# A second buffer for the first-key one-hots, paid for with the tiles of transposed expert numbers

## Chip, core and metric

The kernel runs on one core of one Trainium2 chip. The metric is the device time of one execution in microseconds. The engines are named as in the profile: PE (matrix products), DVE (the vector engine), ACT (activations), POOL (a general engine, which here also issues the gathers), SP (which issues most of the plain loads and stores).

## What is computed

One transformer block for 1024 tokens of width 1024 (and 16 meta tokens): a convolution branch and a latent attention branch, then a channel mixer that picks experts by product keys, then a final norm. Nearly all that matters here is the mixer:

```
s = jnp.einsum('chpd,hpnd->chpn', q, keys)        # two lists of 128 scores per head
sv, si = lax.top_k(s, K)                          # K = 16, 8 heads
...
eidx = jnp.take_along_axis(cidx.reshape(C, PEER_HEADS, K * K), sel, axis=-1)
g = jax.nn.softmax(top_s, axis=-1)
u = u_tab[eidx]                                   # 16384 experts of 1024 numbers
act = jax.nn.gelu(jnp.einsum('chkd,cd->chk', u, xb))
w = g * act
return jnp.einsum('chk,chkd->cd', w, v_tab[eidx])
```

So each token picks 8 x 16 = 128 of the 16384 experts. An expert's number is 128 times its first key plus its second key.

## The kernel before

The 1024 tokens are eight chunks of 128. The mixer is computed in two ways side by side.

**Gather path, chunks 0 to 3.** For each of the 128 picks of a token POOL gathers a row of `u_tab` per token (tile `ug`, 512 KB, line 696), and DVE takes its dot product with the token (`ujunk`, L699). Then rows of `v_tab` are gathered (tile `vg`): for chunks 0 to 2 token by token, summed by PE (`gv`, L736 and L740), for chunk 3 pick by pick, summed by DVE (`ht`, L711 and L713). There are 512 gathers of `u` and 512 of `v`. They are steps of one stream that runs beside the rest of the program.

**Dense path, chunks 4 to 7.** PE computes all 16384 experts for these 512 tokens: `pa` (L180, from `u_t`) and `pv` (L180, into `acc` by DVE at L857). This is the dense part, the second half of the execution. It needs the weights of all experts for each token, most of them zero, and those are made by the **expansion** before it.

**The expansion** (function `expand`, run once per dense chunk, E0 to E3) goes through a chunk in 4 quarters of 32 tokens, and a quarter in 4 pieces of 8 (`r0` = 0, 8, 16, 24), 64 pieces in all. A piece makes four tiles of 128 x 1024 half-precision numbers: `two` (one-hots of the second key), `one` (one-hots of the first key), `ah` = `one` times the high part of the weight, `al` = `one` times the low part. DVE makes them, except that `al` of the pieces with `r0` 8 and 24 is made by POOL. PE multiplies `ah` and `al` with `two` into `pg`, ACT copies that out (`st`), and SP stores it (`g_d`), where the dense part reads it (`gt`). `two`, `ah` and `al` have two buffers each; `one` has one. So the next piece's `one` waits until `ah` and `al` of this piece have been made, on POOL where POOL makes `al`.

**What sets the order.** The program is written as a list of steps (`ORDER`: B attention, C output mix and key scores, S and T the choice of experts, E expansion, G and U gathers and first dense work, D dense part). A scheduler places every instruction by a simulated time when the kernel is built, and so fixes each engine's order; on the chip each engine works through its own list strictly in order and waits by semaphores. What stands between two instructions in a list therefore depends on what the scheduler thought would be ready. POOL's gathers stand in the same list as its `al`, and DVE's dot products in the same list as `two`, `one`, `ah` and the additions into `acc`.

In names such as `one4_1_24` and `vg3_108` the first number is the chunk; then come quarter and `r0`, or the number of the gather.

The function `turn` makes `eT`, a chunk's expert numbers with tokens along the free axis (512 bytes per partition). Chunks 0 to 2 keep it, since their gathers of `v` read it; for chunks 4 to 7 only the two instructions behind it read it. Chunk 3 has none.

Of the kernel before, what the change touches and what calls it, by code (L numbers as in the profile page):

```python
# [17 lines left out]
I32 = mybir.dt.int32  # L18
# [7 lines left out]
P = 128  # L26
# [36 lines left out]
GATHER = [0, 1, 2, 3]  # L63
# [21 lines left out]
def trunk_kernel(ctx, tc, x, meta, g_mix, w_ab, w_lat, g_q, w_uq, g_kv, w_ukv, conv_w, conv_b,  # L85
# [5 lines left out]
    const = ctx.enter_context(tc.tile_pool(name="const", bufs=1))  # L91
# [3 lines left out]
    def bank(name, shape=(P, 512), tag="c"):  # L95
        pool, n, t = banks[tag]
        return pool.tile(list(shape), F32, name=name, tag=t, bufs=n)
# [59 lines left out]
    def transpose_to(dst, src, m):  # L157
        PE.transpose(dst, src, ident[:m, :m])
# [504 lines left out]
    def turn(c):  # L663

        if c in VROWS:
            return
        ef, g = picks[c]
        tp = bank(f"et{c}", (P, 4, P), "s" if c in DENSE else "c")
        transpose_to(tp[:, 0], ef, P)
        eT = const.tile([P, P], I32, name=f"eT{c}", tag="eT", bufs=5)  # L670
        V.tensor_copy(eT, tp[:, 0])
        if c in GATHER:
            chunks[c] += (eT,)
        else:
            transpose_to(tp[:, 1], g.rearrange("p h k -> p (h k)"), P)
            t = sel.tile([P, 4, P], F16, name=f"gd{c}", tag="gd", bufs=len(DENSE))
            A.activation(t[:, 0], tp[:, 1], AF.Copy, scale=GSCALE)
            V.scalar_tensor_tensor(t[:, 1], tp[:, 1], GSCALE, t[:, 0], op0=OP.mult, op1=OP.subtract)
            ii = sel.tile([P, 2, P], I32, name=f"ii{c}", tag="ii", bufs=1)
            V.tensor_scalar(ii[:, 0], eT, 7, None, op0=OP.logical_shift_right)  # L680
            V.tensor_scalar(ii[:, 1], eT, NK - 1, None, op0=OP.bitwise_and)
            V.tensor_copy(t[:, 2:4], ii)
            chunks[c] = t
# [77 lines left out]
    def expand(ci):  # L761

        c = DENSE[ci]
        t = chunks[c]
        for q in range(P // TG):
            st = [ex.tile([P, NK // 2, TG], F32, name=f"st{c}_{q}_{i}", tag="st", bufs=STB) for i in range(2)]
            for r0 in range(0, TG, TH):
                sh = [P, TH // 2, NK, 2]

                def col(r):  # L770
                    cv = t[:, r, q * TG + r0:q * TG + r0 + TH].rearrange("p (a b) -> p a b", b=2)
                    return cv[:, :, None, :].broadcast_to(sh)
                one, two, ah, al = [ex.tile(sh, F16, name=f"{n}{c}_{q}_{r0}", tag=n, bufs=b)
                                    for n, b in (("one", 1), ("two", 2), ("ah", 2), ("al", 2))]
                V.tensor_tensor(two, io[:, None].broadcast_to(sh), col(3), op=OP.is_equal)  # L775
                V.tensor_tensor(one, io[:, None].broadcast_to(sh), col(2), op=OP.is_equal)  # L776
                V.tensor_tensor(ah, one, col(0), op=OP.mult)  # L777
                (G if r0 // TH in ALP else V).tensor_tensor(al, one, col(1), op=OP.mult)
                for r in range(0, TH, 4):
                    pg = bank(f"pg{c}_{q}_{r0}_{r}", (P, 4, NK), "bs"[r // 4 % 2])  # L780
                    for k in range(4):
                        a, b = divmod(r + k, 2)
                        PE.matmul(pg[:, k], two[:, a, :, b], ah[:, a, :, b], start=True, stop=False)  # L783
                        PE.matmul(pg[:, k], two[:, a, :, b], al[:, a, :, b], start=False, stop=True)  # L784
                    for i in range(2):
                        A.activation(st[i][:, :, r0 + r:r0 + r + 4].rearrange("p a b -> p b a"),  # L786
                                     pg[:, :, i * NK // 2:(i + 1) * NK // 2], AF.Copy, scale=1.0 / GSCALE)
            for i in range(2):
                gs = slice(i * NK // 2 // NG, (i + 1) * NK // 2 // NG)
                nc.sync.dma_start(g_d[gs, :, ci * (P // TG) + q].rearrange("g p r -> p g r"),  # L790
                                  st[i].rearrange("p (g a) t -> p g (a t)", a=NG))
# [103 lines left out]
    for t in tops[0]:  # L895
        select(*t)
        turn(t[0])
# [16 lines left out]
    for step in ORDER.split():  # L914
# [8 lines left out]
        elif step[0] == "T":  # L923
            for t in tops[i]:
                turn(t[0])
        elif step[0] == "X":
            bp_ctx.close()
            ex = ex_ctx.enter_context(tc.tile_pool(name="ex", bufs=1, side="right", **RW))
            io = ex.tile([P, NK, 2], F16, name="io")
            G.iota(io, pattern=[[1, NK], [0, 2]], base=0, channel_multiplier=0, allow_small_or_imprecise_dtypes=True)  # L930
        elif step[0] == "Y":
            cp_ctx.close()
            dx = ctx.enter_context(tc.tile_pool(name="dx", bufs=1, **RW))
            XD = (dx.tile([P, KD, ND], F32R, name="xdh"), dx.tile([P, KD, ND], F32R, name="xdl"))
            du = ctx.enter_context(tc.tile_pool(name="du", bufs=1, **RW))
            ges = []
        elif step[0] == "N":
            dense_x()
        elif step[0] == "U":
            ges += [dense_u(k, lambda n: bank(n)) for k in range(i)]  # L940
        elif step[0] == "E":
            expand(i)
        elif step[0] == "D":
            ex_ctx.close()
            sel_ctx.close()
            ps_ctx.close()
            dense()
        else:
            for _ in range(i):
                next(steps)  # L950
# [54 lines left out]
```

## Time and profile before

| | |
|---|---|
| Median of the runs | 2932.6 us (2932.31 to 2934.2, 3 runs) |
| The profiled execution's own time | 2917.6 us |
| Its span, first to last instruction | 2915.8 us |
| Busy: PE / DVE / POOL / ACT | 2495.5 / 2286.2 / 1637.0 / 992.8 us |
| Expansion, first to last of its tiles on DVE | 934.5 to about 1366 us |
| Dense part, first `pv` to last | 1401 to about 2886 us |

All stretches below are microseconds from the start of that span. The span is 1.8 us shorter than the execution's own time, and that is 15 us shorter than the median of the runs; a change is worked out against the profiled execution and then carried to the median. In a row of a timeline the first two numbers are start and duration, and the brackets at the end give the time that the engine sat idle before it and what released it. In a row of waits the numbers are total us, times, and longest.

### The profile page before, as it was taken

To read this page: it belongs to the slowest core of one execution; us is meant where nothing else is said; L and a number is where in the kernel's file an instruction comes from. 1 tells how busy PE (TensorE), PEld (TensorE's weight loads), DVE (VectorE), ACT (ScalarE), POOL (GpSimd) and SP (SyncE) were. 2 spreads that over 40 slices of the span, in tenths; PEclk is the share of its full clock that TensorE was granted. 3 is DMA by queue.
4 is the path that set the end of the run, shared out by engine and by line. 5 is a ranking of instruction groups with operands and counts; after the bars stand their busy time and mean duration, and the time that the engine had idled before them with its cause. 6 is when DMAs were issued, how large, how long until landed. Compare 5 with 4: busy or idle time off the path is not lost.

```text
span 2915.8 us, 39518 instructions
## 1 busy us (share of the span) xinstructions
PE 2495.5 (86%) x12781; PEld 1913.6 (66%) x12781; DVE 2286.2 (78%) x4866; ACT 992.8 (34%) x2176; POOL 1637.0 (56%) x1524
## 2 busy tenths in 40 slices
PE   6878848889795773845799999999999999999996
PEld 6775626767662452534688767777777777778885
DVE  4879767999998689989799966566666565669998
ACT  5436414444440342343333322322222232233232
POOL 5886464453668778766254454454444544545554
PEclk9988959988897886965899999999999999999998
DMA  4113789998797998798999999899999999989996
GB/s 141 53 45 115 227 266 329 315 289 269 230 369 239 350 351 299 242 328 295 326 327 328 339 394 344 325 360 330 348 336 345 338 342 336 344 314 351 348 340 235
DMA packets 373137, 860.40 MB, mean 295 GB/s; under 512 B 38016, under 2 KB 134464, under 8 KB 368832
## 3 DMA queue, kind: packets, MB, share of 16 engines
q0 software_dynamic: 147456, 536.94, 51.3%
q1 hardware_dynamic: 217104, 297.77, 30.2%
q10 hardware_dynamic: 8368, 23.15, 2.2%
q8 instruction: 101, 1.65, 0.2%
q14 instruction: 108, 0.88, 0.1%
HBM read 801.02 MB, written 56.71 MB: 294 GB/s over the span
## 4 chain that ended last, share of the span: by engine, by line
PE 48%; DVE 22%; issue 9%; DMA 9%; POOL 7%; ACT 1%; POOLq 0%; SPq 0%; DVEq 0%; ACTq 0%
PE pv L180 20%; PE pa L180 20%; DMA ug<-in_dram,ei 5%; DVE ujunk L699 5%; PE gv L740 4%; POOL ug L696 2%; DVE eq L642 2%; POOL vg L736 1%; DVE acc L314 1%; DVE ah L777 1%; PE q L588 1%; DVE two L775 1%; DVE one L776 1%; DVE ef L645 1%; DMA vg<-in_dram,eT 1%
## 5 line engine op out<-in xcount | busy, mean ns | idle before, releaser
L696 POOL DMA_INDIRECT ug<-in_dram,ei x512 | 573.1, 1119 | 660.3 <-DVE ujunk L699 464.6
L699 DVE SCALAR_TENSOR_TENSOR ujunk<-ug,xn 128x1024 bf16<-128x1024 f32 x512 | 640.1, 1250 | 63.9 <-DMA ug<-in_dram,ei 60.1
L736 POOL DMA_INDIRECT vg<-in_dram,eT x384 | 444.8, 1158 | 286.1 <-PE gv L740 182.4
L857 DVE TENSOR_TENSOR acc<-acc,pv 128x512 f32<-128x512 f32 x256 | 170.5, 684 | 190.4 <-PE pv L180 190.0
L711 POOL DMA_INDIRECT vg<-in_dram,ei x128 | 170.0, 1328 | 140.3 <-DVE ht L713 106.4
L740 PE MATMUL gv<-vg,wd 128*32 128x512 f32 x1536 | 202.2, 630 | 18.9 <-DMA vg<-in_dram,eT 18.9
L805 ACT ACTIVATE u_1h<-u_1r 128x512 fp32r<-128x512 f32 x128 | 80.7, 631 | 403.7 <-PE pa L180 397.5
L180 PE MATMUL pv<-v_0h,wh 128*128 128x512 f32 x512 | 200.2, 395 | 17.6 <-ACT wh L843 15.4
L180 PE MATMUL pa<-xdh,u_0l 128*128 128x512 f32 x512 | 203.1, 397 | 6.8 <-DVE u_0l L806 6.8
L180 PE MATMUL pa<-xdh,u_0h 128*128 128x512 f32 x512 | 203.2, 397 | 0.2 <-DVE xdl L194 0.2
L180 PE MATMUL pa<-xdl,u_0h 128*128 128x512 f32 x512 | 202.8, 396 | 0.0
L180 PE MATMUL pa<-xdh,u_1h 128*128 128x512 f32 x512 | 200.7, 392 | 0.1
L180 PE MATMUL pa<-xdh,u_1l 128*128 128x512 f32 x512 | 200.0, 391 | 0.3 <-DVE u_1l L806 0.3
L180 PE MATMUL pa<-xdl,u_1h 128*128 128x512 f32 x512 | 200.1, 391 | 0.0
L180 PE MATMUL pv<-v_1h,wl 128*128 128x512 f32 x512 | 198.9, 390 | 0.0
L180 PE MATMUL pv<-v_0l,wh 128*128 128x512 f32 x512 | 198.7, 394 | 0.0
L180 PE MATMUL pv<-v_1l,wh 128*128 128x512 f32 x512 | 198.7, 391 | 0.0
L805 ACT ACTIVATE u_0h<-u_0r 128x512 fp32r<-128x512 f32 x128 | 80.5, 629 | 335.4 <-PE pa L180 308.7
L180 PE MATMUL pv<-v_1h,wh 128*128 128x512 f32 x512 | 194.1, 391 | 0.0
L180 PE MATMUL pv<-v_0h,wl 128*128 128x512 f32 x512 | 193.4, 393 | 0.0
L783 PE MATMUL pg<-ah,two 128*128 128x128 f16 x512 | 92.9, 263 | 108.0 <-DVE ah L777 68.4
L786 ACT ACTIVATE st<-pg 128x256 f32<-128x256 f32 x256 | 130.4, 649 | 149.5 <-PE pg L784 110.4
(454 smaller groups left out, 6061.0 us busy)
## 6 DMA issues: line engine op xcount, KB each, us to landing
g_d<-st SPq DMA_DIRECT2D x32, 1024.0 KB, 13.1
u_0r<-in_dram SPq DMA_DIRECT2D x128, 256.0 KB, 6.1
u_1r<-in_dram SPq DMA_DIRECT2D x128, 256.0 KB, 5.8
gt<-g_d SPq DMA_DIRECT2D x32, 1024.0 KB, 8.5
v_0r<-in_dram SPq DMA_DIRECT2D x128, 256.0 KB, 5.6
v_1r<-in_dram SPq DMA_DIRECT2D x128, 256.0 KB, 5.4
wo<-in_dram SPq DMA_DIRECT2D x80, 256.0 KB, 6.0
wq<-in_dram SPq DMA_DIRECT2D x80, 256.0 KB, 5.6
```

What stands on the lines that cost most here:

```text
L180: PE.matmul(dst, l, r, start=first and j == 0, stop=last and j == 2)
L314: V.scalar_tensor_tensor(acc, hv, cw[:, b, k:k + 1], acc, op0=OP.mult, op1=OP.add)
L642: V.tensor_tensor(eq, tf[:, h:h + hb, ks, None].broadcast_to(sh), iota_c[:, None, None, :n].broadcast_to(sh), op=OP.is_equal)
L696: G.indirect_dma_start(out=ug, out_offset=None, in_=u_tab, in_offset=bass.IndirectOffsetOnAxis(ap=ei[:, j:j + 1], axis=0))
L699: V.scalar_tensor_tensor(junk, ug, 1.0, xn, op0=OP.mult, op1=OP.mult, accum_out=dots[:, j:j + 1])
L711: G.indirect_dma_start(out=vg, out_offset=None, in_=v_tab, in_offset=bass.IndirectOffsetOnAxis(ap=ei[:, j:j + 1], axis=0))
L736: G.indirect_dma_start(out=vg[j], out_offset=None, in_=v_tab, in_offset=bass.IndirectOffsetOnAxis(ap=eT[:, t:t + 1], axis=0))
L740: PE.matmul(acc[32 * j:32 * j + 32, 512 * n:512 * n + 512], w[:, j, 32 * i:32 * i + 32], vg[j][:, 512 * n:512 * n + 512], start=q == 0 and ...
L783: PE.matmul(pg[:, k], two[:, a, :, b], ah[:, a, :, b], start=True, stop=False)
L786: A.activation(st[i][:, :, r0 + r:r0 + r + 4].rearrange("p a b -> p b a"), pg[:, :, i * NK // 2:(i + 1) * NK // 2], AF.Copy, scale=1.0 / G ...
L805: A.activation(hi, raw, AF.Copy)
L857: V.tensor_tensor(a, a, pv, op=OP.add)
```

## The change

`one` gets a second buffer (128 x 1024 numbers of two bytes, 2048 bytes per partition). The five buffers of `eT` become three for the chunks that keep it and a single one, under a tag of its own, for chunks 4 to 7.

```
-        eT = const.tile([P, P], I32, name=f"eT{c}", tag="eT", bufs=5)
+        eT = const.tile([P, P], I32, name=f"eT{c}", tag="eT" if c in GATHER else "eTd", bufs=3 if c in GATHER else 1)
...
                 one, two, ah, al = [ex.tile(sh, F16, name=f"{n}{c}_{q}_{r0}", tag=n, bufs=b)
-                                    for n, b in (("one", 1), ("two", 2), ("ah", 2), ("al", 2))]
+                                    for n, b in (("one", 2), ("two", 2), ("ah", 2), ("al", 2))]
```

No instruction is added or taken away. The scheduler, which sees the second buffer, writes other orders on all engines from the expansion on. DVE's list where the second quarter of chunk 4 ends reads before:

```order
L776 TENSOR_TENSOR one4_1_24_8808<-io_8061,gd4_8573 128x1024
L699 SCALAR_TENSOR_TENSOR ujunk_12456,dots1_11675<-ug1_38_12454,xn1_11673 128x1024
L729 MEMSET wd1_3873 128x4x8
L777 TENSOR_TENSOR ah4_1_24_8810<-one4_1_24_8808,gd4_8573 128x1024
L730 COPY wd1_3873<-wT0_11653 128x4x8
L776 TENSOR_TENSOR one4_2_0_8842<-io_8061,gd4_8573 128x1024
L775 TENSOR_TENSOR two4_2_0_8843<-io_8061,gd4_8573 128x1024
L777 TENSOR_TENSOR ah4_2_0_8844<-one4_2_0_8842,gd4_8573 128x1024
```

and now, where `hs4_0` and `hs4_1` are the normed tokens of chunks 6 and 7, from which their keys' scores are computed:

```order
L776 TENSOR_TENSOR one4_1_24_8808<-io_8061,gd4_8573 128x1024
L776 TENSOR_TENSOR one4_2_0_8842<-io_8061,gd4_8573 128x1024
L777 TENSOR_TENSOR ah4_1_24_8810<-one4_1_24_8808,gd4_8573 128x1024
L775 TENSOR_TENSOR two4_1_24_8809<-io_8061,gd4_8573 128x1024
L577 SCALAR_TENSOR_TENSOR hs4_0_8063<-hs4_0_8063,fs4_0_8182,gffn_3853 128x1024
L699 SCALAR_TENSOR_TENSOR ujunk_12456,dots1_11675<-ug1_38_12454,xn1_11673 128x1024
L776 TENSOR_TENSOR one4_2_8_8872<-io_8061,gd4_8573 128x1024
L729 MEMSET wd1_3873 128x4x8
L730 COPY wd1_3873<-wT0_11653 128x4x8
L577 SCALAR_TENSOR_TENSOR hs4_1_8064<-hs4_1_8064,fs4_1_8202,gffn_3853 128x1024
L777 TENSOR_TENSOR ah4_2_0_8844<-one4_2_0_8842,gd4_8573 128x1024
```

Two `one` now stand one behind the other, and the two norms stand behind `one` of later pieces. The same list at the end of the expansion, before (`ug1_100` is gather 100 of chunk 1, gather 228 of the stream):

```order
L778 TENSOR_TENSOR al7_3_16_10820<-one7_3_16_10817,gd7_9808 128x1024
L775 TENSOR_TENSOR two7_3_24_10848<-io_8061,gd7_9808 128x1024
L699 SCALAR_TENSOR_TENSOR ujunk_14066,dots1_11675<-ug1_100_14064,xn1_11673 128x1024
L776 TENSOR_TENSOR one7_3_24_10847<-io_8061,gd7_9808 128x1024
L699 SCALAR_TENSOR_TENSOR ujunk_14070,dots1_11675<-ug1_101_14068,xn1_11673 128x1024
L777 TENSOR_TENSOR ah7_3_24_10849<-one7_3_24_10847,gd7_9808 128x1024
L699 SCALAR_TENSOR_TENSOR ujunk_14074,dots1_11675<-ug1_102_14072,xn1_11673 128x1024
```

and now:

```order
L776 TENSOR_TENSOR one7_3_24_10847<-io_8061,gd7_9808 128x1024
L775 TENSOR_TENSOR two7_3_16_10818<-io_8061,gd7_9808 128x1024
L699 SCALAR_TENSOR_TENSOR ujunk_13912,dots1_11675<-ug1_92_13910,xn1_11673 128x1024
L777 TENSOR_TENSOR ah7_3_16_10819<-one7_3_16_10817,gd7_9808 128x1024
L778 TENSOR_TENSOR al7_3_16_10820<-one7_3_16_10817,gd7_9808 128x1024
L775 TENSOR_TENSOR two7_3_24_10848<-io_8061,gd7_9808 128x1024
L777 TENSOR_TENSOR ah7_3_24_10849<-one7_3_24_10847,gd7_9808 128x1024
L699 SCALAR_TENSOR_TENSOR ujunk_13916,dots1_11675<-ug1_93_13914,xn1_11673 128x1024
```

Ahead of the last `ah` stood the dot products up to `ug1_101`; now they stand up to `ug1_92`, nine fewer. Everything else that DVE did ahead of that point is the same in number. At the end of the program, around the last addition into `acc` (`pv31_1_3`), DVE's list was:

```order
L857 TENSOR_TENSOR acc_11637<-acc_11637,pv31_1_2_25753 128x512
L713 SCALAR_TENSOR_TENSOR ht3_21846<-vg3_120_24530,dots3_18407,ht3_21846 128x1024
L857 TENSOR_TENSOR acc_11637<-acc_11637,pv31_1_3_25767 128x512
L713 SCALAR_TENSOR_TENSOR ht3_21846<-vg3_121_24533,dots3_18407,ht3_21846 128x1024
L713 SCALAR_TENSOR_TENSOR ht3_21846<-vg3_122_24536,dots3_18407,ht3_21846 128x1024
```

and is now:

```order
L857 TENSOR_TENSOR acc_11637<-acc_11637,pv31_1_2_25753 128x512
L713 SCALAR_TENSOR_TENSOR ht3_21846<-vg3_107_24153,dots3_18407,ht3_21846 128x1024
L857 TENSOR_TENSOR acc_11637<-acc_11637,pv31_1_3_25767 128x512
L713 SCALAR_TENSOR_TENSOR ht3_21846<-vg3_108_24200,dots3_18407,ht3_21846 128x1024
L713 SCALAR_TENSOR_TENSOR ht3_21846<-vg3_109_24203,dots3_18407,ht3_21846 128x1024
```

In both the gathers go on to `vg3_127`, with nothing else between, and then come the five final norms (L758). So 7 gathers stood behind the last addition, and now 20 do.

## Rows read from the trace of the kernel before

**Rows 1.** The page, its first line
```profile
span 2915.8 us, 39518 instructions
```

**Rows 2.** Busy time by stretch: expansion's last part, two of the dense part
```profile
core 0: us, PE busy (x) PEld busy (x) DVE busy (x) ACT busy (x) POOL busy (x), PEclk, DMA share, GB/s
...
1275.00:1366.00 91.00, 39.22 (x333) 32.73 (x331) 90.16 (x124) 42.22 (x85) 56.53 (x39) 0.54 0.87 284
...
2000.00:2400.00 400.00, 400.00 (x1940) 294.34 (x1939) 250.75 (x411) 111.55 (x193) 193.22 (x180) 1.00 0.93 341
...
2589.00:2886.00 297.00, 296.67 (x1317) 243.62 (x1314) 275.51 (x331) 93.12 (x159) 168.67 (x128) 1.00 0.93 333
```

**Rows 3.** Waits of PE in the dense part (1440 to 2886)
```profile
PE pv L180 <- DVE acc L857: 2.2, 2, 1.8
```

**Rows 4.** Waits of DVE in 930 to 1370: total us, times, longest
```profile
DVE one L776 <- POOL al L778: 33.7, 12, 5.7
...
DVE two L775 <- PE pg L784: 0.4, 1, 0.4
```

**Rows 5.** The same wait in three windows: 930 to 1007, 1007 to 1100, 1230 to 1275
```profile
DVE one L776 <- POOL al L778: 15.5, 4, 5.7
...
DVE one L776 <- POOL al L778: 7.9, 5, 2.3
...
DVE one L776 <- POOL al L778: 10.3, 3, 4.2
```

**Rows 6.** Timeline of POOL near 1000: gathers queued ahead of its multiply
```profile
999.20 0.99 POOL L736 DMA_INDIRECT vg<-in_dram,eT  x1 [5.53 <-PE gv L740]
...
1003.94 1.91 POOL L778 TENSOR_TENSOR al<-one,gd 128x1024 f16<-128x1024 f16 x1
```

**Rows 7.** Timeline of DVE and ACT near 1000: second norm, scores, first maximum
```profile
996.24 1.28 DVE L577 SCALAR_TENSOR_TENSOR hs<-hs,fs,gffn 128x1024 f32<-128x1024 f32 x1
...
1006.35 0.69 ACT L599 ACTIVATE s<-s 128x256 f32<-128x256 f32 x2
...
1008.30 0.87 DVE L605 MAX8 sv<-s 128x8 f32<-128x128 f32 x4
```

**Rows 8.** Timeline of POOL and DVE near 1010: what runs under a multiply on POOL
```profile
1010.53 1.89 POOL L778 TENSOR_TENSOR al<-one,gd 128x1024 f16<-128x1024 f16 x1 [3.10 <-DVE one L776]
...
1010.61 0.29 DVE L606 FIND_INDEX8 sx<-sv,s 128x8 uint32<-128x128 f32 x1
...
1011.33 2.18 DVE L699 SCALAR_TENSOR_TENSOR ujunk<-ug,xn 128x1024 bf16<-128x1024 f32 x1
```

**Rows 9.** Timeline of POOL and DVE near 1279: one operation without and with it
```profile
1278.89 2.33 POOL L778 TENSOR_TENSOR al<-one,gd 128x1024 f16<-128x1024 f16 x1 [1.74 <-DVE one L776]
...
1277.46 0.68 DVE L775 TENSOR_TENSOR two<-io,gd 128x1024 f16<-128x1024 f16 x1
...
1279.38 2.38 DVE L775 TENSOR_TENSOR two<-io,gd 128x1024 f16<-128x1024 f16 x1
```

**Rows 10.** All multiplies of POOL by tile al (durations: least, median, most)
```profile
L778 POOL TENSOR_TENSOR al<-one,gd x32: 1888/1908/2874, 955.1 to 1362.7; 128x1024 f16<-128x1024 f16 x32
```

**Rows 11.** Timeline of DVE near 1290: two dot products back to back
```profile
1290.01 1.21 DVE L699 SCALAR_TENSOR_TENSOR ujunk<-ug,xn 128x1024 bf16<-128x1024 f32 x1
...
1291.26 1.22 DVE L699 SCALAR_TENSOR_TENSOR ujunk<-ug,xn 128x1024 bf16<-128x1024 f32 x1
```

**Rows 12.** Timeline of DVE, the end
```profile
2890.75 9.21 DVE L713 SCALAR_TENSOR_TENSOR ht<-vg,dots,ht 128x1024 f32<-128x1024 f32 x7
...
2909.27 1.28 DVE L758 SCALAR_TENSOR_TENSOR acc<-acc,os,gfin 128x1024 f32<-128x1024 f32 x1 [0.44 <-POOL os L143]
```

**Rows 13.** Timeline of POOL, one of its last gathers
```profile
2886.54 0.94 POOL L711 DMA_INDIRECT vg<-in_dram,ei  x1 [0.30 <-issue]
```

**Rows 14.** Gathers of the rows path in 2589 to 2900, by line
```profile
L711 POOL DMA_INDIRECT vg<-in_dram,ei x128 | 170.0, 1328 | 140.3 <-DVE ht L713 106.4 <-PE gv L740 20.8 <-issue 12.2
```

**Rows 15.** Gathers by tile vg: issue to landing
```profile
DMA to landing us min/median/max: 4.2/7.1/13.0
```

## The prediction, as recorded before the run

> **What bounds the kernel now.** I read the page first, then busy time by stretch, then the waits of one engine in one stretch, then the timeline at the places where those waits lie. The span is 2915.8 us [rows 1]. Its second half is the dense part, and there PE is the bound: it is busy 400.00 of 400 us in one stretch and 296.67 of 297 in another, at a granted clock of 1.00 [rows 2], and its only wait for DVE in all of it is 2.2 us [rows 3]. So the dense part keeps its length, and it ends earlier by as much as it starts earlier. Two other things set the end: when the expansion is through, and how many gathers are left when PE has finished. In the last part of the expansion DVE is the bound, 90.16 of 91 us, while PE runs at about half its clock and is busy less than half the time [rows 2]. At the very end DVE goes through 7 more gathers in 9.21 us, and then the final norms follow [rows 12].
>
> The wait that the change aims at is plain: in the expansion DVE waits 12 times, 33.7 us in all, with `one` for POOL's `al` [rows 4]. In the same stretch `two` waits 0.4 us for PE [rows 4].
>
> **The change, part by part.** *The eT tiles* cost nothing: one conversion per dense chunk now waits until two 0.3 us operations on the chunk before have run, and these stand right behind the conversion on the same engine. Were they in the way, it would be under 1 us, three times.
>
> *Term A, nine dot products leave the expansion.* DVE's list has nine fewer `ujunk` ahead of the last `ah`. Back to back two of them start 1.25 us apart [rows 11], so DVE, which is the bound there, is through 9 x 1.25 = 11.2 us sooner. I take this in full, since the last 91 us have hardly a gap [rows 2].
>
> *Term B, what of the 33.7 us comes back.* I split the wait by what POOL does in it. `al` on POOL takes 1.9 us [rows 10], and ahead of it POOL issues gathers: the `al` at 1003.94 stands behind gathers of which the first had waited 5.53 us for PE [rows 6]. The share that is `al` itself is not free for DVE. While POOL runs an `al` from 1278.89, DVE's `two` takes 2.38 us, where one just before it took 0.68 [rows 9]. An `al` from 1010.53 makes a dot product take 2.18 us where 1.22 is usual [rows 8, 11], though a search for the index of a maximum ran beneath it in its usual 0.29 [rows 8]. So if DVE doesn't wait for `al`, its next operation is held up by it all the same, unless it is one of the searches.
>
> By windows [rows 5]: four waits in 930 to 1007 make 15.5 us. They hold at most 4 x 1.9 = 7.6 us of `al`, which leaves 7.9 us that POOL spent in its queue. But little of it can move the rest. The next long piece of DVE's work is the searches on the scores of chunks 6 and 7, and these need the second norm, which DVE made at 996.24, then PE and ACT; ACT had the first scores at 1006.35 + 0.69 = 1007.0, and DVE began on them at 1008.30 [rows 7]. In the new list that norm stands behind `one4_2_8`, which takes over the buffer of `one4_1_24` and so needs that piece's `al` from POOL. POOL's list up to there holds the same gathers and one `al` more, so I take it that the norm comes no sooner than it came, and the scores neither. DVE then gains the 1.3 us between 1007.0 and 1008.30 and the 0.6 us of a `one` made in advance. I take 2 us.
>
> The five waits in 1007 to 1100 make 7.9 us, 1.6 each, which is less than one `al`: nothing but the lock. There, though, about half of DVE's list are searches, which run beneath it. I take 3 of 7.9.
>
> The three waits in 1230 to 1275 make 10.3 us, of which 3 x 1.9 = 5.7 are `al`; the other 4.6 I take in full, for in the new list DVE has four dot products to do between a `one` and the next that must wait. From 1275 on there is no such wait at all, since what `al` costs there is already in DVE's busy time.
>
> Sum 2 + 3 + 4.6 = 9.6. With two buffers `ah` and `two` come close behind the piece that PE has yet to finish, where their waits were 0.4 us [rows 4]; 0.6 us for that leaves B = 9. Its bounds are 0 (every wait only moves) and 33.7 (the lock costs nothing); between the two I stay near the 7.9 + 4.6 = 12.5 us that are queueing, less what the scores forbid.
>
> *Term C, thirteen gathers move behind the end of PE.* Behind the last addition DVE's list now has 20 gathers where it had 7, so 13 more. DVE alone takes 9.21 / 7 = 1.32 us for each [rows 12], which gives 13 x 1.32 = 17.1 us. Those 7 had all been issued ahead, while DVE was held up by other work. With 20 to go POOL must keep up: its issues took 1.33 us on average in this phase [rows 14], and 0.30 us lie between two when nothing holds it [rows 13], 1.63 in all, which gives 13 x 1.63 = 21.2. A single undisturbed issue took 0.94 [rows 13], which would be 1.24 with the gap. I take 1.5 us, between the DVE row and the POOL row, since POOL is quicker when DVE stands waiting: C = 19.5. A gather lands 7.1 us after its issue [rows 15]; `vg` has eight buffers, at 1.3 us each more than that, so the landing is covered.
>
> The Trainium skill, on its page "SBUF — State Buffer" (section "Who interferes with whom"), says that a DVE instruction with two SBUF inputs contends with a GpSimd instruction that reads SBUF, and that one with a single input doesn't. The stretched dot product and the unhurt search agree with it, and by it alone, with no search in DVE's way, B could not pass the 12.5 us of queueing. The same section infers that `tensor_tensor` takes the shared pair's read side only and the writing of a gather's descriptors the other; by this DVE's additions would not slow POOL, C would be 17.1 and the sum about 2.4 us lower. The average of 1.33 us against an undisturbed 0.94 doesn't fit that.
>
> **The sum.** - 11.2 - 9 + 19.5 = -0.7 us. On the profiled execution, 2917.6 us by its own time, that is 2916.9. That execution lies 15 us under the median of the runs; carried to the median, 2932.6 - 0.7 gives 2931.9 us. What the expansion gives is taken back by gathers which the same scheduler, seeing a shorter expansion, moved out of it.
>
> **The rivals.** 0.2% is 5.9 us, about what a measurement can tell from no change.
>
> *Faster: the queue was the trouble, not the multiply.* If the order of POOL's list lets `al` fall under searches or under time in which DVE has nothing to do, more of the 33.7 us comes back. It decides from 19.5 - 11.2 + 5.9 = 14.2 us on. With B = 20 the time is 2932.6 - 11.2 - 20 + 19.5 = 2921; with all of it and C at 17.1 it is 2905. For it speaks that the waits are real gaps on an engine that is the bound after 1006; against it the rows on the lock, and that the scores of chunks 6 and 7 hold the first half. Chance 0.35.
>
> *Slower: the wait only moves, and the tail stays.* The new lists put two `al` of POOL close together and `one` further forward, so that DVE may reach the next `one` as early against POOL as it did. Place: the norm of chunk 6, which stood ahead of such a `one` and now stands behind it; every us lost there is lost on the scores. Then B is 0 or a little under, and with C at 21.2 the sum is 21.2 - 11.2 = +10, 2943 us. It decides when B falls below 2.4 us (19.5 - 11.2 - 5.9). For it: thirteen gathers in the tail are certain by the lists, while B is not. Against it: the three waits near 1250 have nothing ahead of them that could take their place. Chance 0.27.
>
> *The change doesn't act,* since the lock gives DVE nothing and the gathers taken from the expansion return at the end: that is my forecast, taken to its limit (B = 8.3 gives zero). No change by more than 0.2%: chance 0.38.
>
> **The numbers.** The forecast is 2931.9 us. Its own range, with B from 3 to 12.5 and C from 17.1 to 21.2, goes from 2932.6 - 11.2 - 12.5 + 17.1 = 2926.0 to 2932.6 - 11.2 - 3 + 21.2 = 2939.6. The faster case goes down to 2905; I leave out its lower half, and start at 2917. The slower one ends at 2943, and 2 us more for a wait that I don't see: 2945. Faster 0.35, same 0.38, slower 0.27.
>
> **What the next profile would show.** Term A: the last `ah` of the expansion ends some 20 us earlier than 1365 us. Term B: the wait of `one` for `al` falls from 33.7 us to under 10, no wait is left near 1250, and the operations of DVE that run beside an `al` are stretched to some 2.4 us in place of it; the first searches on the scores of chunk 6 still begin near 1006. Dense part: PE full and as long as before, its last `pv` some 20 us earlier than 2886. Term C: after the last addition into `acc` 20 gathers in 26 to 30 us, in place of 7 in 9.2, with DVE waiting for gathers at the end of them. I am wrong if the dense part changes its length (then the shift of the gathers acts on PE or on the DMA queues, which I have left out), if the tail's gathers take other than 1.3 to 1.6 us each, or if new waits of DVE for PE or ACT of more than a few us stand in the expansion.

## The result: slower by 0.55%, and the profile after

The changed kernel takes 2947.1 us (median of 5 runs, 2943.3 to 2955.8) against 2932.6 us before (also 5 runs, 2932.3 to 2934.2): a ratio of 1.0055, 95% interval 1.0042 to 1.0067. That is 14.5 us between the medians. The forecast was 2931.9 us with a range to 2945; the time lies just outside the range, on the side of the slower rival. The profiled execution took 2947.1 us, and its span is 2945.3 us, against 2915.8 [rows 1].

First the tail. Timeline of DVE at the end of the changed kernel (start, duration, engine, line, operation):

```profile
2902.52 0.68 DVE L857 TENSOR_TENSOR acc<-acc,pv 128x512 f32<-128x512 f32 x1
2903.12 26.37 DVE L713 SCALAR_TENSOR_TENSOR ht<-vg,dots,ht 128x1024 f32<-128x1024 f32 x20
...
2938.79 1.28 DVE L758 SCALAR_TENSOR_TENSOR acc<-acc,os,gfin 128x1024 f32<-128x1024 f32 x1 [0.44 <-POOL os L143]
```

Twenty gathers stand behind the last addition, in 26.37 us, where 7 took 9.21 [rows 12]: 17.2 us more, 1.32 a gather. POOL keeps up:

```profile
2908.16 1.02 POOL L711 DMA_INDIRECT vg<-in_dram,ei  x1 [0.30 <-issue]
2909.49 1.01 POOL L711 DMA_INDIRECT vg<-in_dram,ei  x1 [0.30 <-issue]
```

One issue and the 0.30 us behind it make 1.32 to 1.33, the pace of DVE, whose 20 additions follow one another without a wait for a gather. PE is as full in the dense part as it was [rows 2, 3]; its waits there (1450 to 2910) are:

```profile
PE pv L180 <- DVE acc L857: 5.6, 4, 2.9
```

Now the expansion. The rows by tile give the first and last start of an operation (after the three durations in ns). In the changed kernel:

```profile
L775 DVE TENSOR_TENSOR two<-io,gd x64: 665/679/2770, 945.3 to 1371.9; 128x1024 f16<-128x1024 f16 x64
...
L777 DVE TENSOR_TENSOR ah<-one,gd x64: 633/679/5068, 949.1 to 1372.5; 128x1024 f16<-128x1024 f16 x64
...
L857 DVE TENSOR_TENSOR acc<-acc,pv x256: 671/684/690, 1421.2 to 2902.5; 128x512 f32<-128x512 f32 x128
```

From the first `two` to the last `ah` it takes 1372.5 - 945.3 = 427.2 us. All that follows uses this measure, "the expansion", with the start of the last `ah` to that of the last addition as "the dense part" (here 1530.0 us). Two runs with the lists of the kernel before give the same measure: its own profile, 934.5 to 1363.0, is 428.5, and the first experiment below 427.6. So the expansion gained some 1 us, where terms A and B (nine dot products fewer, and the wait for POOL's `al`) promised 20.2.

The waits of DVE in the expansion (940 to 1380) show why at a glance, against [rows 4]:

```profile
DVE one L776 <- POOL al L778: 10.4, 4, 4.6
DVE ah L777 <- PE pg L783: 8.6, 3, 7.3
DVE ah L777 <- PE pg L784: 7.9, 4, 2.2
DVE sv L605 <- ACT s L599: 5.9, 4, 2.7
DVE ah L777 <- remote: 5.4, 1, 5.4
```

The wait that the change aims at fell from 33.7 us to 10.4. But `ah`, which hardly waited before, waits 21.9 us (8.6 + 7.9 + 5.4). All of it is a wait for PE: what the profile calls "remote" ended, by the trace, on PE's semaphore too, with a count that belongs to no recorded product. The prediction had named such new waits of DVE as a sign that it is wrong.

### The profile page after: what moved, and what is told of

Its sections match the earlier page's. It is cut to its first block, busy times and chain, and to the rows that moved or that the text cites. A ratio compares the mean times of both kernels' runs of the same rounds, so it can differ in the third digit from the quotient of the medians.

```text
span 2945.3 us, 39531 instructions
## 1 busy us (share of the span) xinstructions
PE 2502.0 (85%) x12781; PEld 1914.8 (65%) x12781; DVE 2304.2 (78%) x4866; ACT 990.5 (34%) x2176; POOL 1623.2 (55%) x1524
## 4 chain that ended last, share of the span: by engine, by line
PE 46%; DVE 9%; issue 4%; DMA 4%; POOL 2%; ACT 0%; POOLq 0%; SPq 0%; DVEq 0%; another core or an unknown queue 0%; ACTq 0%
PE pv L180 20%; PE pa L180 20%; PE gv L740 4%; DMA ug<-in_dram,ei 3%; DVE ujunk L699 2%; POOL ug L696 1%; DVE ah L777 1%; DVE ht L713 1%; DVE two L775 1%; PE q L588 1%; DVE one L776 1%; DVE al L778 1%; DMA g_d<-st 1%; PE pg L784 0%; DMA v_0r<-in_dram 0%
## 5 line engine op out<-in xcount | busy, mean ns | idle before, releaser
L699 DVE SCALAR_TENSOR_TENSOR ujunk<-ug,xn 128x1024 bf16<-128x1024 f32 x512 | 649.1, 1268 | 62.9 <-DMA ug<-in_dram,ei 58.6
L736 POOL DMA_INDIRECT vg<-in_dram,eT x384 | 427.0, 1112 | 269.9 <-PE gv L740 164.5
L740 PE MATMUL gv<-vg,wd 128*32 128x512 f32 x1536 | 204.7, 638 | 14.4 <-DMA vg<-in_dram,eT 12.3
```

Source lines behind the costliest of these rows:

```text
L699: V.scalar_tensor_tensor(junk, ug, 1.0, xn, op0=OP.mult, op1=OP.mult, accum_out=dots[:, j:j + 1])
L736: G.indirect_dma_start(out=vg[j], out_offset=None, in_=v_tab, in_offset=bass.IndirectOffsetOnAxis(ap=eT[:, t:t + 1], axis=0))
L740: PE.matmul(acc[32 * j:32 * j + 32, 512 * n:512 * n + 512], w[:, j, 32 * i:32 * i + 32], vg[j][:, 512 * n:512 * n + 512], start=q == 0 and ...
```

## The experiments

The kernel before ran beside each group of runs, on the same chip; since its median differs from group to group (2925 to 2933 us), runs are compared by their ratios to it.

### 1. The eT tiles alone

```diff
-        eT = const.tile([P, P], I32, name=f"eT{c}", tag="eT", bufs=5)
+        eT = const.tile([P, P], I32, name=f"eT{c}", tag="eT" if c in GATHER else "eTd", bufs=3 if c in GATHER else 1)
```

> The kernel before with the split of the eT tiles alone; one buffer of `one`. Every engine's list of instructions is the same as before, word for word. Theory (the tail: thirteen more gathers behind the last addition cost 17 us, and the expansion gives back only 3): the split is free, 2932.6 us within 2 us, and the first `two` starts where it does in the kernel before on this chip. Rival (something ahead of the expansion, by where tiles lie or by the wait of an eT conversion, costs the 10.8 us by which the first `two` of the changed kernel is later in its trace): 2940 to 2944 us, with the first `two` at 945 us rather than 934.5.

Measured: 2933.0 us, ratio 1.0008 (0.9996 to 1.0019). The split is free. The run is also the kernel before once more, since its lists are the same, and its rows by tile are:

```profile
L775 DVE TENSOR_TENSOR two<-io,gd x64: 668/682/3027, 948.8 to 1372.9; 128x1024 f16<-128x1024 f16 x64
...
L777 DVE TENSOR_TENSOR ah<-one,gd x64: 664/683/2814, 952.0 to 1376.4; 128x1024 f16<-128x1024 f16 x64
...
L857 DVE TENSOR_TENSOR acc<-acc,pv x256: 672/683/689, 1425.6 to 2905.6; 128x512 f32<-128x512 f32 x128
```

The first `two` starts at 948.8 here, at 934.5 in the profile of before and at 945.3 in that of the changed kernel, with the same instructions ahead of it in all three. Nor does it go by the split: two runs below without it (experiments 2 and 5) start at 943.6 and 943.0, one with it (experiment 7) at 934.7. So the 10.8 us by which the changed kernel's trace is late there are no effect of the change, and the 15 us that the profile of before lies under its own median arose there too. From that point on this run and the profile of before agree: expansion 427.6 and 428.5, dense part 1529.2 and 1527.2. It is the better partner for the changed kernel, and is called "the partner" below.

### 2 and 3. Five buffers of ge, with one and with two of one

```diff
-GEB = 6
+GEB = 5
...
-                                    for n, b in (("one", 1), ("two", 2), ("ah", 2), ("al", 2))]
+                                    for n, b in (("one", 2), ("two", 2), ("ah", 2), ("al", 2))]
```

`ge` takes the results of `pa` on their way to the weights (`wh`) that `pv` needs. The first run has the first line of the edit, the second both; in both the eT tiles keep their five buffers.

> The kernel before with 5 buffers of `ge` in place of 6, which makes room for a second `one` without touching eT; `one` still has one buffer. Its list of DVE has no gather behind the last addition, where the kernel before has 7. It is the partner of the next run. Theory (the tail counts 1.32 us a gather): 7 x 1.32 = 9.2 us less, 2923 us, unless a fifth buffer of `ge` is missed, which would show as PE waiting for `ge` in the dense part. Rival (gathers moved out of the tail lengthen the dense part by as much): 2932 us.

> The run before with a second buffer of `one` and nothing else (eT keeps its five buffers). The last `ah` has 222 dot products ahead of it in DVE's list where the partner has 230, and 3 gathers stand behind the last addition where the partner has none. Theory (the tail decides; the second buffer itself brings 3 us in the expansion): partner + 4.0 - 3 = 1 us over the partner. Rival 1 (the second buffer costs by itself, in the expansion or the dense part, and the tail only adds): 6 to 15 us over the partner. Rival 2 (the prediction's 20 us of gain in the expansion are real, but were lost to something particular in the changed kernel): 16 us under the partner.

Measured: 2937.3 us, ratio 1.0022 (1.0009 to 1.0035), and 2948.8 us, 1.0062 (1.0043 to 1.0081). The numbers of both theories missed on the first: the tail is empty, but the dense part is 1541.9 us, 12.7 longer than the partner's. The difference begins ahead of the first `pv`, where PE waits for the first `wh`, in the partner and in this run:

```profile
PE pv L180 <- ACT wh L843: 15.4, 1, 15.4
...
PE pv L180 <- ACT wh L843: 30.9, 1, 30.9
```

Between the last `ah` and that `pv` the partner's PE makes 72 products of `pa`; with five `ge` it makes none there, and they come later. With two `one` the expansion is 426.9 us against 427.0 with one: no gain, as in the changed kernel. The second run is 11.5 us slower by the medians, which is in the range of its first rival (a cost in the expansion or the dense part). It lies in the dense part. The trace has 10.4 us more there and 6.3 more behind the last addition; PE's wait of `pv` for `acc` goes from 2.8 to 9.0 us. (Together that is more than 11.5, since the first run's profiled execution was the fastest of its ten.) The scheduler rearranged the dense part as well, so the pair is a clean comparison for the expansion alone.

### 4 and 5. All al on DVE, with two and with one of one

```diff
-ALP = [1, 3]
+ALP = []
```

`ALP` lists the pieces of a quarter, counted from 0, whose `al` POOL makes. The first run is the changed kernel with this line, the second the kernel before with it.

> The changed kernel with all `al` on DVE, none on POOL, so no wait for POOL's `al` is possible and no DVE operation runs beside one. DVE gets 32 more `al`, 32 x 0.68 = 22 us. 22 gathers stand behind the last addition (20 in the changed kernel). Theory (a POOL `al` holds up whatever DVE runs beside it, so that removing a wait only moves the price into stretched operations): the ah, al, u_l and eq that now take 1.0 to 1.5 us go back to 0.6 to 0.7, and 30 to 45 us of stretching leave DVE along with 27 us of waits, against 22 us of new work; the expansion is 10 to 40 us shorter and the time 2910 to 2940 us. Rival (the stretching is no price of the POOL `al`, or is under searches for the most part): 22 us of new work on the engine that is the bound, 2955 to 2970 us.

> The kernel before with all `al` on DVE: one buffer of `one`, five of eT, so the last run without the change. 234 dot products ahead of the last `ah` (222 in the last run), 7 gathers behind the last addition (22 there). Theory (POOL's `al` is what cost DVE time, whichever way `one` is buffered, so without it the second buffer is worth nothing): 15 x 1.32 = 19.8 us less in the tail, up to 12 x 1.25 = 15 us more in the expansion (416 us from the first `two` to the last `ah`, against 401 in the last run), 2901 to 2916 us. Rival (the second buffer of `one` is what shortened the expansion in the last run): an expansion of 425 us or more, and 2922 us or more.

Measured: 2920.6 us, ratio 0.9964 (0.9953 to 0.9976), and 2909.9 us, ratio 0.9949 (0.9933 to 0.9964). Both beat the kernel before and the changed one. In the first, DVE has 32 operations more, and the expansion is 400.5 us, 26.7 shorter than the changed kernel's. Rows by tile of the second:

```profile
L775 DVE TENSOR_TENSOR two<-io,gd x64: 639/686/728, 943.0 to 1351.1; 128x1024 f16<-128x1024 f16 x64
...
L777 DVE TENSOR_TENSOR ah<-one,gd x64: 637/689/704, 946.2 to 1355.8; 128x1024 f16<-128x1024 f16 x64
```

The longest `two` is now 0.73 us and the longest `ah` 0.70; beside an `al` of POOL they took up to 2.65 and 2.81 in the run of experiment 1. (Its 3.03 us `two` ran beside another multiplication of POOL, for `ep`; that one remains, and here it holds a `one` for 5.29 us.) The expansion is 1355.8 - 943.0 = 412.8. Between these two runs lie 12 dot products (222 and 234), and 412.8 - 400.5 = 12.3 us, 1.03 each, less than the 1.25 between two of them back to back [rows 11]. So nothing is left for the second `one`: without POOL's `al` it is worth nothing. DVE still waits for PE with `ah`, 24.3 us in the first run and 25.6 in the second; the largest of these rows, first run, then second:

```profile
DVE ah L777 <- PE pg L783: 20.9, 2, 19.1
...
DVE ah L777 <- PE pg L783: 25.6, 4, 16.1
```

What 32 `al` on POOL cost DVE, by waits and by what ran beside them, follows from the partner: 427.6 - 412.8 = 14.8 us, though the new run does 4 dot products (4.1 us) and 32 `al` (32 x 0.686 = 22.0) more. That makes 40.9 us, 1.3 for each `al` that POOL takes over, for 0.69 saved.

### 6. Multiplications on POOL that nobody waits for

```diff
-                (G if r0 // TH in ALP else V).tensor_tensor(al, one, col(1), op=OP.mult)
+                V.tensor_tensor(al, one, col(1), op=OP.mult); r0 // TH in ALP and G.tensor_tensor(ex.tile(sh, F16, name=f"scr{c}_{q}_{r0}", tag="scr", bufs=1), io[:, None].broadcast_to(sh), col(1), op=OP.mult)
```

The eT tiles are split as well, to make room for `scr`; otherwise this is the kernel of experiment 5.

> The run before with 32 multiplications added on POOL, of the same shape and place in the program as the `al` that POOL made in the kernel before, but into a scratch tile that nobody reads, from a constant and the gates: no engine ever waits for one. (eT is split as in the changed kernel, to make room for the tile; `one` has one buffer.) 227 dot products ahead of the last `ah` where the partner has 234, and 14 gathers in the tail where it has 7; these two would cancel, - 7 x 1.25 + 7 x 1.32. Theory (a POOL multiplication costs DVE time by running, not by being waited for): 0.8 to 1.5 us each, 32 of them 26 to 48 us, over the partner's time, in stretched `two`, `ah`, `al` and dot products, with no wait of DVE for POOL's `al`. Rival (it is the wait and the buffers that cost): within 6 us of the partner.

Measured: 2947.2 us, ratio 1.0073 (1.0054 to 1.0091), 37 us over the last run. The expansion is 436.3 us, 23.5 longer with 7 dot products fewer: some 31 us at 1.03 each, or 1.0 for each of the 32. No operation reads `scr`, and DVE has no wait for POOL's L778. Groups of DVE in its expansion (times, busy us, mean ns):

```profile
L775 DVE TENSOR_TENSOR two<-io,gd 128x1024 f16<-128x1024 f16 x64 | 57.8, 904 | 3.3 <-POOL io L930 3.3
L778 DVE TENSOR_TENSOR al<-one,gd 128x1024 f16<-128x1024 f16 x64 | 56.3, 879 | 0.0
L777 DVE TENSOR_TENSOR ah<-one,gd 128x1024 f16<-128x1024 f16 x64 | 53.2, 832 | 9.9 <-PE pg L783 9.3
```

and in that of the run without them:

```profile
L778 DVE TENSOR_TENSOR al<-one,gd 128x1024 f16<-128x1024 f16 x64 | 43.9, 686 | 0.0
L777 DVE TENSOR_TENSOR ah<-one,gd 128x1024 f16<-128x1024 f16 x64 | 43.9, 686 | 26.1 <-PE pg L783 25.6
L775 DVE TENSOR_TENSOR two<-io,gd 128x1024 f16<-128x1024 f16 x64 | 43.9, 687 | 5.3 <-POOL io L930 3.3 <-PE pg L784 1.9
```

The three groups grew by 35.6 us together, and 16.3 us of a wait of `ah` for PE went away under that. One of them, from the two engines' timeline:

```profile
1280.04 2.60 DVE L777 TENSOR_TENSOR ah<-one,gd 128x1024 f16<-128x1024 f16 x1
...
1280.19 1.90 POOL L778 TENSOR_TENSOR scr<-io,gd 128x1024 f16<-128x1024 f16 x1
```

### 7. A third ah, under five ge and two one

```diff
-                                    for n, b in (("one", 2), ("two", 2), ("ah", 2), ("al", 2))]
+                                    for n, b in (("one", 2), ("two", 2), ("ah", 3), ("al", 2))]
```

It is the second run of experiments 2 and 3 with this line, and with the eT tiles split.

> The run with 5 buffers of `ge` and 2 of `one`, with a third buffer of `ah` (and eT split, which was free). 222 dot products ahead of the last `ah` and 3 gathers in the tail, both as there. It takes away what makes `ah` wait for PE, 22 us in the changed kernel. Theory (waits and stretching are two forms of one price, set by POOL's multiplications): the waits of `ah` for PE go, DVE's operations beside `al` get longer by as much, and the expansion stays within 5 us of 427.5; 2944 to 2953 us. Rival (the change moved the wait to the ring of `ah`, one buffer further would have paid): the expansion is 12 to 20 us shorter, 2929 to 2937 us.

Measured: 2931.4 us, ratio 1.0025 (1.0013 to 1.0036), where the run with two `ah` has 1.0062. The expansion is 419.7 us, against 426.9. The theory missed: the ring of `ah` has a share of its own, 7 us, though not the 12 to 20 of the rival, and `ah` still waits 15.5 us for PE. The lists of the two runs differ in more than the ring, so the 7 us are of the ring and of the new order together.

### 8. Half as many al on POOL

```diff
-ALP = [1, 3]
+ALP = [1]
```

> The changed kernel with every fourth `al` on POOL (16 of 64) in place of every second (32); two buffers of `one`. 222 dot products ahead of the last `ah`, 21 gathers in the tail. Theory (each POOL `al` costs DVE the same, more than the 0.68 us that it saves): half way between the changed kernel and the one with all `al` on DVE, an expansion of about 414 us and 2934 us. Rival (the cost comes from two POOL `al` close together with one pair of buffers; with one to a tile and two `one` it is hidden): each saves DVE 0.68 us, 16 x 0.68 = 11 us, an expansion of 390 us and 2910 us.

Measured: 2932.2 us, ratio 1.0021 (1.0011 to 1.0032). The expansion is 415.5 us, where the changed kernel has 427.2 and the one with none on POOL 400.5: near the middle, 413.9. `ah` waits 33.8 us for PE here. The ratio is somewhat above the middle of theirs, 1.0010.

### 9 and 10. The room for a third ah in place of a second one

```diff
-                                    for n, b in (("one", 2), ("two", 2), ("ah", 2), ("al", 2))]
+                                    for n, b in (("one", 1), ("two", 2), ("ah", 3), ("al", 2))]
```

The first is the changed kernel with this line, the second has all `al` on DVE besides.

> The room that the change gives to a second `one` goes to a third `ah` in its place: eT split, one buffer of `one`, three of `ah`, POOL's `al` as before. 229 dot products ahead of the last `ah` (before 230), 11 gathers in the tail (before 7). Theory (POOL's multiplications set the price, and rings only choose where it is paid): the expansion stays at 428 to 432 us, the tail grows by 4 x 1.32 = 5.3 us, 0.1 to 0.3% slower than the kernel before. Rival (the ring of `ah` is short by itself, as the 7 us suggest that a third `ah` took from the expansion in the run with five `ge`): an expansion of 418 to 424 us, and 0 to 0.2% faster than before.

> The best run so far (one buffer of `one`, all `al` on DVE; 0.9949 of the time before) with a third buffer of `ah`, in the room of the split eT. 232 dot products ahead of the last `ah` (234 there), 7 gathers in the tail as there. Theory (with POOL's `al` gone, what is left to gain is the 25.6 us that `ah` waits for PE): the expansion 5 to 15 us shorter than 413.5, a ratio of 0.990 to 0.993. Rival (PE is late there for reasons of its own, ahead of it in its queue, and DVE waits as long one piece later): the expansion within 4 us of 411 (two dot products fewer), a ratio of 0.994 to 0.996.

Measured: 2941.7 us, ratio 1.0031 (1.0016 to 1.0045), with an expansion of 426.6; and 2921.8 us, 0.9968 (0.9956 to 0.9979), with 413.7. The ring of `ah` alone gives 1 us, where under a second `one` it came with 7 (experiment 7). Without POOL's `al` it gives nothing, and the rival holds for the expansion, though the ratio lies a little above its range: PE is late for reasons of its own, and the wait for it stands at `two` in place of `ah`, 14.4 and 11.7 us (the "remote" is PE's semaphore again).

```profile
DVE two L775 <- remote: 14.4, 3, 7.4
DVE two L775 <- PE pg L784: 11.7, 7, 4.3
```

### 11. Fills on POOL in place of multiplications

```diff
-                (G if r0 // TH in ALP else V).tensor_tensor(al, one, col(1), op=OP.mult)
+                V.tensor_tensor(al, one, col(1), op=OP.mult); r0 // TH in ALP and G.memset(ex.tile(sh, F16, name=f"scr{c}_{q}_{r0}", tag="scr", bufs=1), 0.0)
```

As in experiment 6, the eT tiles are split.

> As the run with 32 multiplications on POOL that nobody reads, but each is a fill of the scratch tile with zeros, which reads nothing from SBUF. 233 dot products ahead of the last `ah`, 8 gathers in the tail; the partner without any of it has 234 and 7, and 0.9949 of the time before. The Trainium skill, page SBUF — State Buffer, section Who interferes with whom, says that a DVE instruction with two SBUF inputs contends with a GpSimd instruction that reads SBUF; by that the fills cost DVE nothing, and the time is within 5 us of the partner's. In the rows of these runs alone: theory (it is the reading of operands by POOL that DVE is held up by) a ratio of 0.994 to 0.997, DVE operations beside a fill at their usual 0.68 us; rival (any POOL operation at that place costs DVE, by its duration) stretched `two` and `ah` beside the fills, and a ratio of 0.999 or more if a fill takes as long as half a multiplication.

Measured: 2926.9 us, ratio 0.9979 (0.9964 to 0.9994), between the bounds of the two theories. The trace decides for the first: a fill takes 0.95 us (half a multiplication), and the 26 operations of DVE for `two`, `one`, `ah` and `al` that ran beside one took 0.66 to 0.69 us. (Three others took 1.8 to 3.5, beside POOL's multiplications for `ep`.) From the timelines of DVE and POOL:

```profile
1005.38 0.69 DVE L777 TENSOR_TENSOR ah<-one,gd 128x1024 f16<-128x1024 f16 x1
1005.99 0.68 DVE L778 TENSOR_TENSOR al<-one,gd 128x1024 f16<-128x1024 f16 x1
...
1005.20 0.96 POOL L778 MEMSET scr<- 128x1024 f16 x1
```

The expansion is 415.7 us, 2.9 over the run without fills, where the multiplications of experiment 6 added 23.5. The rest of the difference lies in the dense part (1528.7 against 1524.9) and one more gather in the tail. So the trace agrees with the Trainium skill, page "SBUF — State Buffer", section "Who interferes with whom": what counts is whether GpSimd's instruction reads SBUF.

### 12. The tail cut back to seven gathers

```diff
-        for j in range(P):
+        for j in range(P - 13):
```

It is the loop of `gather_v_rows`, so the rows of chunk 3 leave out 13 experts; the rest is the changed kernel.

> The changed kernel without the last 13 of the 128 gathers and additions of chunk 3 (its rows lack those 13 experts), so that 7 stand behind the last addition, as in the kernel before; the lists are otherwise the changed kernel's. It leaves the expansion with the second `one` as the only difference to the kernel before. Theory (of the changed kernel's 0.55%, the tail is 13 x 1.32 = 17.2 us and the rest a small gain of the expansion): 17 us under the changed kernel, 2930 us, a ratio to the kernel before of 0.997 to 1.001. Prediction on record (the expansion gains 20 us): a ratio of 0.993. Rival (the tail overlaps with something else that ends as late): a ratio above 1.002.

Measured: 2929.5 us, ratio 1.0000 (0.9988 to 1.0011). Without the 13 gathers in the tail the changed kernel is as fast as the kernel before, to 0.1%. So the whole loss is the tail; the second `one`, with all that the scheduler made of it in the expansion, gives nothing that can be measured. The expansion is 425.0 us here, the dense part 1528.7.

## Why the prediction was wrong, step by step

**The eT tiles**: free, as said (experiment 1).

**The base.** The profile of before lay 15 us under the median, ahead of the expansion (experiment 1). Carrying the sum over to the median was right.

**Term C, the tail**: the mechanism was right and the size 2.3 us too large, 17.2 us against 19.5. The measured value is that of the lower bound, the row of DVE, because POOL's issues, at 1.02 us each and not the 1.33 of their average in the dense part [rows 14], kept to 1.32 with the gap. The prediction had expected DVE to wait for gathers at the end, and it did not. POOL's pace agrees with the inference of the Trainium skill (page "SBUF — State Buffer", section "Who interferes with whom") on the writing of descriptors, by which C would be 17.1; the page makes it for `tensor_tensor`, and the additions here are `scalar_tensor_tensor`.

**Term A, nine dot products**: no run has it by itself. Between experiments 4 and 5 a dot product is worth 1.03 us (12.3 us for 12), if the second `one` is worth nothing there; the prediction took 1.25.

**Term B is the step that failed.** It was put at 9 us gained. The expansion takes 427.2 and 425.0 us in the changed kernel and in experiment 12, against 428.5 and 427.6 with the lists of before: 2 us less in the mean, not 20.2 (with five `ge` it is 0.1, experiments 2 and 3). With A between 9 x 1.03 = 9.3 and the 11.2 of the prediction, B was a loss of 7 to 9 us. The sum with what was measured, -2.0 + 17.2 = 15.2 us, agrees with the 14.5 us between the medians.

By chunk it can be seen where. The expansion has four chunks of 16 `two` each; windows from the first `two` of a chunk to that of the next, the last one to the last `ah` (the window, its length, then busy us of PE, its weight loads, DVE, ACT and POOL, the granted clock and the DMA's share and GB/s), in the partner:

```profile
948.82:1070.15 121.33, 91.00 (x592) 64.81 (x591) 102.87 (x243) 40.76 (x87) 92.37 (x70) 0.82 0.96 343
1070.15:1224.28 154.13, 90.92 (x569) 61.28 (x571) 142.32 (x422) 50.03 (x99) 126.82 (x92) 0.76 0.80 274
1224.28:1306.51 82.23, 49.52 (x383) 33.38 (x375) 67.57 (x104) 37.60 (x77) 51.05 (x39) 0.79 0.97 329
1306.51:1376.35 69.84, 29.76 (x240) 24.32 (x240) 69.67 (x97) 30.69 (x60) 42.48 (x31) 0.50 0.89 299
```

and in the changed kernel:

```profile
945.32:1075.47 130.15, 92.20 (x591) 65.34 (x589) 100.59 (x244) 38.54 (x81) 95.53 (x73) 0.84 0.94 326
1075.47:1223.39 147.92, 87.99 (x568) 59.95 (x570) 141.57 (x413) 50.38 (x104) 97.24 (x83) 0.77 0.83 273
1223.39:1310.35 86.96, 52.74 (x382) 36.37 (x374) 76.84 (x110) 39.01 (x78) 57.77 (x46) 0.71 0.94 318
1310.35:1372.46 62.11, 26.87 (x231) 23.58 (x232) 62.11 (x81) 28.42 (x56) 35.39 (x24) 0.57 0.89 274
```

DVE's dot products in these stretches are 17, 19, 14 and 22 before, 17, 16, 16 and 14 after. The last chunk is 7.7 us shorter for 8 dot products fewer: no more than term A. The second is 6.2 shorter for three fewer, and the third 4.7 longer for two more, where one `u_l` and one reduction into `ef` (other work of DVE) have gone from the one to the other as well: work moved, and no gain from the wait. The third still holds a wait of `one` for POOL's `al` of 4.64 us, which ends at 1263.04; the prediction had taken the waits near there as gone. The first has the same 17, and is 8.8 us longer; experiment 12 repeats it (129.8 us), and so does the run with five `ge` and two `one` (129.4, with one `one` 122.5).

What happens in the first chunk is on the timelines of DVE, PE and POOL near 1010 of the changed kernel:

```profile
1009.60 1.27 DVE L577 SCALAR_TENSOR_TENSOR hs<-hs,fs,gffn 128x1024 f32<-128x1024 f32 x1
1018.21 0.69 DVE L777 TENSOR_TENSOR ah<-one,gd 128x1024 f16<-128x1024 f16 x1 [7.34 <-PE pg L783]
...
1002.01 0.26 PE L784 MATMUL pg<-al,two 128*128 128x128 f16 x1 [5.45 <-POOL al L778]
...
1003.59 3.64 PE L740 MATMUL gv<-vg,wd 128*32 128x512 f32 x16
...
1012.53 4.79 PE L588 MATMUL q<-nt,wq 128*128 128x256 f32 x16
1017.15 0.22 PE L783 MATMUL pg<-ah,two 128*128 128x128 f16 x1
...
1000.06 1.90 POOL L778 TENSOR_TENSOR al<-one,gd 128x1024 f16<-128x1024 f16 x1
```

With a second `one` DVE goes one piece further ahead and comes to the ring of `ah`, two deep. The next `ah` needs products that PE has behind the transposes and queries of the second norm. PE itself had stood still 5.45 us for POOL's `al` just before. So the wait did not go away: it went from `one`, for POOL, to `ah`, for PE. POOL's `al` is not what makes PE late in general, for with none on POOL `ah` waits as long (24.3 and 25.6 us, experiments 4 and 5). In the first chunk DVE waits 12.2 us for `al` in the partner; in the changed kernel it waits 4.0 for `al` and 19.4 for PE in `ah`. For that wait the prediction had allowed 0.6 us, by the 0.4 us that `two` had waited for PE [rows 4]. That row was of a kernel in which DVE was held up at `one`, by POOL's `al`, before it got there. The prediction was right that the scores of chunk 6 would come no sooner: DVE's first search on them starts 75.6 us behind the first `two` (1020.93 - 945.32), before 73.8.

Over the four windows DVE stands idle 46.0 us in the changed kernel and 45.1 in the partner: as much wait came as went. It is busy 381.1 us and 382.4, only 1.3 less, though nine dot products take 9 x 1.22 = 11.0 [rows 11]. The other 9.7 went into operations that took longer. That is what the prediction calls the lock: a multiplication on POOL holds up an operation of DVE with two inputs that runs beside it. The two groups for `u_l`, for example, 15 operations in either kernel, take 18.7 us, where the partner has 12.0. The longest `ah` of the changed kernel, 5.07 us by the row above, is one of two that start at 949.14, beside two multiplications of POOL for `ep` (timelines of DVE and POOL):

```profile
949.14 5.67 DVE L777 TENSOR_TENSOR ah<-one,gd 128x1024 f16<-128x1024 f16 x2
...
949.84 4.41 POOL L644 TENSOR_TENSOR ep<-eq,cidx 128x640 f32<-128x640 f16 x2
```

Which operations are hit also changes: over the expansion `ah` and `al` on DVE take 98 us in the changed kernel and 83 in the partner, while `two` and `eq` take 61 and 76, the same sum of 158 us.

**The rivals.** The slower one had the right shape: the tail stays and the wait only moves, with the second norm as its place. It put B at 0 or a little under, and 2943 us; B was -7 to -9, C lower, and the time 2947. Its reason (two `al` close together on POOL) was not what the trace shows. The share of the ring and that of the lock can't be fully separated: a third `ah` brought 7 us under a second `one` (experiment 7), the lock costs 1.0 to 1.3 us for each POOL multiplication (experiments 5 and 6), and how much of the 8.8 us in the first chunk comes from the new order of PE's list rather than from the ring stays open, since the scheduler changes the order of all engines with each ring.

## What to carry to other kernels

A buffer that removes a wait is worth something only if the engine then meets nothing else; look at the next ring and at the next engine's queue, and don't take the small wait of today as its price, since the wait that is removed is what keeps it small. Here a larger cost than the wait stood beside it: work handed to POOL to relieve DVE cost DVE 1.0 to 1.3 us for each 0.69 saved, and taking it back (one line, experiment 5) gave 0.5%. Where a scheduler orders the program, compare its lists at the end as well: thirteen gathers moved behind the last addition were the whole loss.

## What the runs showed of the hardware

A POOL multiplication reading SBUF held up a DVE operation with two inputs for as long as it ran (2.60 us for an `ah` that takes 0.69), though neither waits for the other in the program (experiment 6). By the trace the `ah` had even started first, at 1280.04 against 1280.19, and POOL took its usual 1.90 us. A fill of the same tile, 0.95 us, did not hold one up (experiment 11). The first `two` came at 934.5, 945.3 and 948.8 us in three executions (kernel before, changed kernel, experiment 1) with the same instructions ahead of it, while the expansion that follows agreed within 1 us between the two of them that have the same lists.
